# Two transformer blocks on one core: weight chunks issued ahead of the norm vectors' rows, and a later start of the modulation product

## The chip, the cores and the metric

The kernel runs on one core of a Trainium2 chip. The metric is the device time of one execution in microseconds (us); the time before is a median of three runs. An engine is called by its short name: PE is TensorE, DVE is VectorE, ACT is ScalarE, POOL is GpSimd, SP is SyncE, which here issues DMA transfers.

## The reference

Input `x` has 256 rows of 1024 values, fp32. The first block is an RMS norm, one wide product with `w_in` that is cut into ten parts, a recurrent branch and a sparse attention branch, a merge, and a gated FFN. The second block runs two layers with a modulation (`c @ w_mod + b_mod`) of norm outputs, and a second stream of 256 context rows (`ctx`) beside the main rows.

```python
def first_block(x, norm_mix_pre, w_in, ...):
    for l in range(DEPTH):
        h = rms_norm(x, norm_mix_pre[l])
        proj = h @ w_in[l]
        ...
        xr, gr, q, k, v, iq, ik, iw, g_a, g_b = parts
        ...
        iq = partial_rope(iq.reshape(bsz, s, N_IDX_HEADS, IDX_DIM), IDX_ROT_DIM)
        ik = layer_norm(ik, idx_k_ln_g[l], idx_k_ln_b[l])
        ik = partial_rope(ik[:, :, None, :], IDX_ROT_DIM)[:, :, 0, :]
        ...
def second_block(x, c, ctx, c_ctx, w_mod, b_mod, ...):
    for l in range(DEPTH_2):
        mod = (silu_c @ w_mod[l] + b_mod[l])[:, None, :]
        mod_c = (silu_cc @ w_mod[l] + b_mod[l])[None, None, :]
        ...
        h = modulate(x, g_pre_mix[l], sh_m, sc_m)
        hc = modulate(ctx, g_pre_mix[l], csh_m, csc_m)
```

## The kernel before

Every product is fp32 accuracy out of three fp32r matmuls: a weight chunk is loaded raw (`mraw`, up to 128x1024), ACT writes its rounded half `mhi` (L319) and DVE the remainder `mlo` (L320); the activations are split in the same way into `xTh` and `xTl`. `wraw` (L173) issues the load on SP's queue and `wload` (L178) takes a chunk that was loaded ahead, if there is one, and splits it. Three `mraw` buffers and three pairs of halves are in rotation. The instructions of each engine are put in a row by a scheduler that works from the program's order, the dependences and its own estimate of times; engines then run their rows strictly in order.

At the begin SP issues the two tiles of `x` (L92), the constant table `tab` (L94, it holds the identity for transposes, the rope tables and masks) and the rows of seven norm and gate vectors (`columns`, L104 to L118, name `vc`). Each is a DMA of 4 to 16 KB into one 128x128 tile, which PE transposes (L114) and ACT copies (L116). Then come three chunks of `w_in` that are loaded ahead (L613, `ahead`): they are for columns 3584 to 3876, the first half of the index projection `pidx`. DMAs use eight completion semaphores in turn, so each one also waits until the eighth before it has landed. `norm_T` (L614) squares `x` on ACT, takes the power -0.5 on POOL (`rs`, L336), scales on DVE (`xn`, L347), transposes on PE (L354), multiplies with the norm vector on DVE and ACT alternately (`mod`, L369 and L366) and splits into `xTh` and `xTl`. A second set of vector rows, `v2` (L617), holds the condition vector `c`.

The index projection (L683) makes two halves of 292 columns with `prod_x`; ACT evacuates each (L687). Then for both row tiles DVE applies rope to the query part (L509 to L512), and the key part `ik` goes through a layer norm (DVE L696, L699, ACT square, DVE `ms` L334, POOL `rs` L336, DVE L702, L703), rope and a copy (L705); PE transposes both (L711, L716) and multiplies them (L728). The next product is that of k, from column 3072 of `w_in`.

`Side` (L129) hands out steps of a generator: `tick(us)` is called by each product with an estimate of its time, adds it to `due`, and runs a step whenever `due` has reached `every`. The modulation (L519) is such a generator, 49 steps of one 512 KB chunk of `w_mod` (`wraw` tile, L536) and its matmuls (L554) each; it starts at L631 with `every` 4.2 and an extra `tick(8.4)`. During the FFN of the first block the context rows' projection and attention (`ctx_project`, L1238) are the generator, one step per 9.5, started at L1262; `side.finish()` (L1267) runs what is left. In an attention (`attend`), for each pair of heads, stage_a makes scores (L1040) and a softmax on DVE and ACT (`Pm`), and stage_b transposes (L1075), copies (`PTm`) and multiplies with the values (L1088). The boundary (L1275) closes the FFN with a norm and starts the next layer's products. The context's output projection `down_f` (L1291) is 96 matmuls of fhi, flo with cah, cal; the scheduler puts them where it sees room.

```python
    W = T["w_in"][0]
    ahead += [wraw(wview(W, k, min(3, 8 - k), 3584, 292), min(3, 8 - k), 292, "m") for k in (0, 3, 6)]
    xh, xl = norm_T(x, vc[:, O_GM:O_GM + 8], None, "m", "D")
    ...
    side.start(modulation(0, wmx.enter_context(tc.tile_pool(name="wm", bufs=1, side="right")), mods[0]), 4.2)
    side.tick(8.4)
    ...
    side.start(ctx_project(cres), 9.5)
```

Of the kernel before, what the change touches and what calls it, by code (L numbers as in the profile page):

```python
# [59 lines left out]
def tile_two_blocks(ctx: ExitStack, tc: tile.TileContext, T, out, dbg=None):  # L60
    nc = tc.nc
# [16 lines left out]
    def bank(tag, name="pb"):  # L78
        return ps.tile([P, 512], F32, tag=tag, name=name, bufs=NB[tag])
# [21 lines left out]
    mhalf = cst.tile([P, 32], F32, name="mhalf")  # L101
    nc.vector.memset(mhalf, -0.5)

    def columns(name, parts):  # L104
        rows = cst.tile([P, P], F32, tag="rows", name=name + "_r")
        nc.vector.memset(rows, 0.0)
        offs, r = [], 0
        for src in parts:
            n = src.shape[0]
            nc.sync.dma_start(rows[r:r + n, :], src)  # L110
            offs.append(r)
            r += n
        pt = bank("F", name + "_p")
        nc.tensor.transpose(pt[:, :P], rows, ident)  # L114
        cols = cst.tile([P, P], F32, name=name)
        nc.scalar.activation(cols, pt[:, :P], AF.Copy)  # L116
        return cols, offs

    def vrows(a):
        return a.rearrange("(r p) -> r p", p=P)  # L120

    cw = T["conv_w"][0].rearrange("k (r p) -> (k r) p", p=P)
    vc, o1 = columns("vc", [vrows(T["norm_mix_pre"][0]), vrows(T["norm_ffn_pre"][0]), cw,
                            vrows(T["conv_b"][0]), vrows(T["rg_b_a"][0]), vrows(T["rg_b_x"][0]),
                            vrows(T["rg_lambda"][0])])
    O_GM, O_GF, O_CW, O_CB, O_BA, O_BX, O_LAM = o1


    class Side:  # L129

# [25 lines left out]
    side = Side()  # L156
# [16 lines left out]
    def wraw(src, a, b, s):  # L173
        raw = wpool[s].tile([P, CH[s]], F32, tag=s + "raw", name=s + "raw", bufs=RAWB[s])
        nc.sync.dma_start(raw[:, :a * b].rearrange("p (a b) -> p a b", a=a), src)
        return raw
# [17 lines left out]
    def wview(W, k0, kn, c0, n):  # L194
        return W[k0 * P:(k0 + kn) * P, c0:c0 + n].rearrange("(k p) n -> p k n", p=P)
# [143 lines left out]
    def wide(s, name):  # L339
        return (apool[s].tile([P, 8, S], F32R, tag=s + "xTh", name=name + "h"),  # L340
                apool[s].tile([P, 8, S], F32R, tag=s + "xTl", name=name + "l"))
# [34 lines left out]
    def norm_T(src, A, B, s, tag):  # L376
        xh, xl = wide(s, "xT")
        if s == "f":
            t2 = apool[s].tile([P, 2, D], F32, tag="ftmp", name="xn2")
        for i in range(2):  # L380
            t = t2[:, i] if s == "f" else ap_.tile([P, D], F32, tag="mtmp", name="xn", bufs=2)
            norm_tile(src[:, i], i, A, B, s, tag, xh, xl, t)
        return xh, xl
# [36 lines left out]
    def gain_row(src, name, s="m"):  # L420
        g = apool[s].tile([P, D], F32, tag=s + "G", name=name, bufs=1)
        nc.sync.dma_start(g, bc_row(src, D))
        return g
# [90 lines left out]
    def modulation(l, wmp, res, accs=None):  # L514
# [87 lines left out]
        for r_ in range(2):  # L602
            A = cst.tile([P, 2, 8], F32, name=f"A{l}{r_}")
            for f_, og in ((0, O_PM), (1, O_PF)):
# [4 lines left out]
    mods = [[], []]  # L609


    W = T["w_in"][0]
    ahead += [wraw(wview(W, k, min(3, 8 - k), 3584, 292), min(3, 8 - k), 292, "m") for k in (0, 3, 6)]  # L613
    xh, xl = norm_T(x, vc[:, O_GM:O_GM + 8], None, "m", "D")  # L614


    v2, o2 = columns("v2", [T["g_pre_mix_2"].rearrange("l (r p) -> (l r) p", p=P),  # L617
                            T["g_pre_ffn_2"].rearrange("l (r p) -> (l r) p", p=P),
                            vrows(T["we_pool_scale_2"][0]), vrows(T["c_2"][0]), vrows(T["c_ctx_2"])])
    O_PM, O_PF, O_PS, O_C, O_CC = o2  # L620
    assert O_CC == O_C + 8
    sil = cst.tile([P, 16], F32, name="sil")
# [5 lines left out]
                                sil.rearrange("p (r k) -> p r k", r=2), 0.5)  # L628

    wmx = ExitStack()  # L630
    side.start(modulation(0, wmx.enter_context(tc.tile_pool(name="wm", bufs=1, side="right")), mods[0]), 4.2)  # L631
    side.tick(8.4)


    bax = ExitStack()
# [305 lines left out]
    xh, xl, rows = boundary_ffn(dn.y, 0.5, gpost1, vc[:, O_GF:O_GF + 8], None, 2, (lws[:2], lws[2:]))  # L941
# [451 lines left out]
    xh, xl, rows = boundary_ffn(dn.y, 1.0, gain_row(Gm, "gm1"), Af, Bf, 2, (lws[:2], lws[2:]))  # L1393
# [40 lines left out]
```

## Time and profile before

| what | us |
|---|---|
| median of three runs | 1435.92 (1435.72 to 1436.95) |
| the profiled execution | 1434.95 |
| its span in the trace | 1433.2 |
| PE busy | 1377.9 (96%) |
| DVE busy | 1003.7 (70%) |
| ACT busy | 719.7 (50%) |
| POOL busy | 39.1 (3%) |

The span runs from the first to the last instruction of the trace; 1.75 us of the execution lie outside it. The profiled execution was 0.97 us shorter than the median. A line of the timeline gives start, duration, engine, source line, operation, tiles and, in brackets, how long the engine was idle before it and what ended that. Matmul records overlap, since matmuls are pipelined: the distance of two starts is the rate. "SPq" rows are DMA issues on SP. A few matmul records can be missing from a trace.

### The profile page before, as it was taken

To read this page: it belongs to the slowest core of one execution; us is meant where nothing else is said; L and a number is where in the kernel's file an instruction comes from. 1 tells how busy PE (TensorE), PEld (TensorE's weight loads), DVE (VectorE), ACT (ScalarE), POOL (GpSimd) and SP (SyncE) were. 2 spreads that over 40 slices of the span, in tenths; PEclk is the share of its full clock that TensorE was granted. 3 is DMA by queue.
4 is the path that set the end of the run, shared out by engine and by line. 5 is a ranking of instruction groups with operands and counts; after the bars stand their busy time and mean duration, and the time that the engine had idled before them with its cause. 6 is when DMAs were issued, how large, how long until landed. Compare 5 with 4: busy or idle time off the path is not lost.

```text
span 1433.2 us, 25321 instructions
## 1 busy us (share of the span) xinstructions
PE 1377.9 (96%) x9852; PEld 1219.2 (85%) x9852; DVE 1003.7 (70%) x1972; ACT 719.7 (50%) x1330; POOL 39.1 (3%) x58
## 2 busy tenths in 40 slices
PE   6999999999999999989999999999999999999997
PEld 5887888979999987866899999999678866899997
DVE  4877955476666656787778776687888886555555
ACT  4567743445554555667532222322677676444443
POOL 1000000000000000001000000000000000000000
PEclk9999999999999999999999999999999999999999
DMA  7763799957566552631467556666374510256663
GB/s 249 227 178 89 222 280 286 264 176 228 170 179 207 166 157 88 206 111 58 148 201 219 177 178 197 185 204 189 117 233 150 175 45 18 86 177 191 181 187 118
DMA packets 296576, 247.90 MB, mean 173 GB/s; under 512 B 11445, under 2 KB 275257, under 8 KB 296457
## 3 DMA queue, kind: packets, MB, share of 16 engines
q1 hardware_dynamic: 296456, 246.30, 56.5%
q8 instruction: 77, 1.26, 0.4%
q14 instruction: 43, 0.34, 0.1%
HBM read 245.18 MB, written 1.08 MB: 172 GB/s over the span
## 4 chain that ended last, share of the span: by engine, by line
PE 84%; DVE 6%; ACT 4%; DMA 3%; issue 2%; POOL 1%; SPq 0%; POOLq 0%; DVEq 0%; ACTq 0%
PE pb L215 15%; PE pb L220 15%; PE pb L219 15%; PE pb L230 9%; PE pb L234 9%; PE pb L233 9%; PE pb L1088 2%; PE pb L554 2%; PE pb L1040 2%; DMA mraw<-in_w_in_dram 2%; PE pb L1082 1%; DVE mlo L320 1%; PE pb L354 1%; POOL rs L336 1%; ACT mhi L319 1%
## 5 line engine op out<-in xcount | busy, mean ns | idle before, releaser
L320 DVE TENSOR_TENSOR mlo<-mraw,mhi 128x1024 fp32r<-128x1024 f32 (+2 forms) x297 | 360.8, 1218 | 246.4 <-ACT mhi L319 243.1
L319 ACT ACTIVATE mhi<-mraw 128x1024 fp32r<-128x1024 f32 (+2 forms) x297 | 312.1, 1054 | 422.1 <-PE pb L219 199.2
L215 PE MATMUL pb<-xTh,mhi 128*128 128x256 f32 x1616 | 461.2, 285 | 0.0
L220 PE MATMUL pb<-xTh,mlo 128*128 128x256 f32 x1616 | 458.6, 284 | 1.6 <-DVE mlo L320 1.4
L219 PE MATMUL pb<-xTl,mhi 128*128 128x256 f32 x1616 | 458.8, 284 | 0.0
L215 PEld LDWEIGHTS pb<-xTh,mhi 128*128 128x128 f32 x1616 | 309.6, 192 | 12.4 <-issue 7.8
L220 PEld LDWEIGHTS pb<-xTh,mlo 128*128 128x128 f32 x1616 | 309.6, 192 | 3.6 <-DVE mlo L320 2.6
L219 PEld LDWEIGHTS pb<-xTl,mhi 128*128 128x128 f32 x1616 | 309.8, 192 | 2.8 <-DVE xTl L320 0.3
L575 DVE SCALAR_TENSOR_TENSOR acc<-wraw,sst,acc 128x1024 f32<-128x1024 f32 x84 | 104.5, 1280 | 6.2 <-DMA wraw<-in_w_mod_dram 6.0
L230 PE MATMUL pb<-mhi,fh 128*128 128x512 f32 x264 | 104.1, 395 | 0.0
L233 PE MATMUL pb<-mlo,fh 128*128 128x512 f32 x264 | 103.5, 392 | 0.0
L234 PE MATMUL pb<-mhi,fl 128*128 128x512 f32 x264 | 102.9, 390 | 0.0
L230 PE MATMUL pb<-mhi,xTh 128*128 128x256 f32 (+1 forms) x272 | 79.9, 295 | 3.9 <-ACT xTh L319 2.4
L233 PE MATMUL pb<-mlo,xTh 128*128 128x256 f32 (+1 forms) x272 | 80.3, 296 | 1.8 <-DVE mlo L320 1.8
L234 PE MATMUL pb<-mhi,xTl 128*128 128x256 f32 (+1 forms) x272 | 80.8, 297 | 0.0
L320 DVE TENSOR_TENSOR flo<-fraw,fhi 128x512 fp32r<-128x512 f32 x92 | 62.7, 688 | 15.2 <-ACT fhi L319 13.0
L319 ACT ACTIVATE fhi<-fraw 128x512 fp32r<-128x512 f32 x92 | 57.0, 625 | 21.9 <-PE pb L234 11.0
L230 PEld LDWEIGHTS pb<-mhi,xTh 128*128 128x128 f32 x272 | 53.5, 197 | 6.7 <-ACT xTh L319 2.8
L234 PEld LDWEIGHTS pb<-mhi,fl 128*128 128x128 f32 x264 | 49.6, 188 | 11.2 <-DVE fl L320 0.5
L230 PEld LDWEIGHTS pb<-mhi,fh 128*128 128x128 f32 x264 | 49.8, 189 | 10.2 <-ACT fh L319 1.1
L233 PEld LDWEIGHTS pb<-mlo,xTh 128*128 128x128 f32 x272 | 53.5, 197 | 4.5 <-DVE mlo L320 3.0
L233 PEld LDWEIGHTS pb<-mlo,fh 128*128 128x128 f32 x264 | 49.8, 189 | 8.4 <-issue 0.4
(403 smaller groups left out, 2339.9 us busy)
## 6 DMA issues: line engine op xcount, KB each, us to landing
wraw<-in_w_mod_dram SPq DMA_DIRECT2D x96, 512.0 KB
mraw<-in_w_ffn_in_dram SPq DMA_DIRECT2D x84, 512.0 KB
mraw<-in_w_in_dram SPq DMA_DIRECT2D x44, 512.0 KB
mraw<-in_w_ffn_out_dram SPq DMA_DIRECT2D x44, 512.0 KB
mraw<-in_w_ffn_down_dram SPq DMA_DIRECT2D x22, 512.0 KB
fraw<-in_w_ffn_out_dram SPq DMA_DIRECT2D x44, 256.0 KB
mraw<-in_w_ffn_gate_dram SPq DMA_DIRECT2D x20, 512.0 KB
mraw<-in_w_ffn_up_dram SPq DMA_DIRECT2D x20, 512.0 KB
```

The source lines that it names most:

```text
L215: ins = nc.tensor.matmul(dst, wh, xh[:, k], start=(k == 0), stop=False)
L219: nc.tensor.matmul(dst, wh, xl[:, k], start=False, stop=False)
L220: ins = nc.tensor.matmul(dst, wl, xh[:, k], start=False, stop=(k == 7))
L230: ins = nc.tensor.matmul(dst, xh_k, wh, start=first, stop=False)
L233: nc.tensor.matmul(dst, xh_k, wl, start=False, stop=False)
L234: return nc.tensor.matmul(dst, xl_k, wh, start=False, stop=last)
L319: return (nc.scalar.activation(hi, src, AF.Copy), nc.vector.tensor_sub(lo, src, hi.bitcast(F32)))
L320: nc.vector.tensor_sub(lo, src, hi.bitcast(F32)))
L554: ins = nc.tensor.matmul(pb[32 * q:32 * q + 32, h * 256:(h + 1) * 256], lhs, rhs[:, q], start=first, stop=last, tile_position=(0, 32 * q), ...
L575: ins = nc.vector.scalar_tensor_tensor(acc[:, r_], raw, col, acc[:, r_], OP.mult, OP.add)
L1040: nc.tensor.matmul(sb[j][:, n * S:(n + 1) * S], qs[a][hd, i * P:(i + 1) * P], keys[n][b][hd, kv, :], start=(m == 0), stop=(m == 2))
L1088: nc.tensor.matmul(ob[64 * j:64 * j + 64, :S], vals[k // 2](k % 2, kv), pts[j][:, k], start=(k == 0), stop=(k == 2 * nb - 1), skip_group_c ...
```

## The change

It does three things. `columns` takes the queue that issues its rows, and `vc` is given ScalarE's (`nc.scalar`), `v2` keeps SP's. The call for `vc` stands behind the three loads ahead. The modulation starts with `due` at -4.1 and `every` 4.1, in place of an extra tick of 8.4 and `every` 4.2.

```diff
-    def columns(name, parts):
+    def columns(name, parts, queue):
...
-            nc.sync.dma_start(rows[r:r + n, :], src)
+            queue.dma_start(rows[r:r + n, :], src)
...
-    vc, o1 = columns("vc", [vrows(T["norm_mix_pre"][0]), vrows(T["norm_ffn_pre"][0]), cw,
-                            vrows(T["conv_b"][0]), vrows(T["rg_b_a"][0]), vrows(T["rg_b_x"][0]),
-                            vrows(T["rg_lambda"][0])])
-    O_GM, O_GF, O_CW, O_CB, O_BA, O_BX, O_LAM = o1
...
     ahead += [wraw(wview(W, k, min(3, 8 - k), 3584, 292), min(3, 8 - k), 292, "m") for k in (0, 3, 6)]
+    vc, o1 = columns("vc", [vrows(T["norm_mix_pre"][0]), vrows(T["norm_ffn_pre"][0]), cw,
+                            vrows(T["conv_b"][0]), vrows(T["rg_b_a"][0]), vrows(T["rg_b_x"][0]),
+                            vrows(T["rg_lambda"][0])], nc.scalar)
+    O_GM, O_GF, O_CW, O_CB, O_BA, O_BX, O_LAM = o1
...
-                            vrows(T["we_pool_scale_2"][0]), vrows(T["c_2"][0]), vrows(T["c_ctx_2"])])
+                            vrows(T["we_pool_scale_2"][0]), vrows(T["c_2"][0]), vrows(T["c_ctx_2"])], nc.sync)
...
-    side.start(modulation(0, wmx.enter_context(tc.tile_pool(name="wm", bufs=1, side="right")), mods[0]), 4.2)
-    side.tick(8.4)
+    side.start(modulation(0, wmx.enter_context(tc.tile_pool(name="wm", bufs=1, side="right")), mods[0]), 4.1)
+    side.due = -4.1
```

The scheduler answers with new rows on every engine. Lines of the changed kernel are 5 lower up to L608 and 1 lower behind it. Three places matter here.

At the begin, on SP's queue (DMA issues; `mraw` is a chunk of `w_in`, `v_r` holds the rows of `v2`), before:

```order
L110 DMA vc_r<-in_rg_b_x_dram 8x128
L110 DMA vc_r<-in_rg_lambda_dram 8x128
L175 DMA mraw<-in_w_in_dram 128x3x292 x2
L175 DMA mraw<-in_w_in_dram 128x2x292
L110 DMA v_r<-in_g_pre_mix_dram 16x128
L110 DMA v_r<-in_g_pre_ffn_dram 16x128
```

and now, from `tab` on:

```order
L94 DMA tab<-in_c_tab_dram 128x960
L170 DMA mraw<-in_w_in_dram 128x3x292 x2
L170 DMA mraw<-in_w_in_dram 128x2x292
L110 DMA v_r<-in_g_pre_mix_dram 16x128
L110 DMA v_r<-in_g_pre_ffn_dram 16x128
```

The first three chunks of `w_in` stand right behind `tab`. Further on in the same queue (`wraw` is a chunk of `w_mod`, `gp` and `bm` are rows of the modulation), before:

```order
L522 DMA gp<-in_g_post_ffn_dram 2x512 x2
L536 DMA wraw<-in_w_mod_dram 128x4x256 x2
L548 DMA bm<-in_b_mod_dram 2x512 x4
L536 DMA wraw<-in_w_mod_dram 128x4x256
L679 DMA lng<-in_idx_k_ln_g_dram 128x64
L680 DMA lnb<-in_idx_k_ln_b_dram 128x64
L536 DMA wraw<-in_w_mod_dram 128x4x256 x2
L175 DMA mraw<-in_w_in_dram 128x3x292 x2
L175 DMA mraw<-in_w_in_dram 128x2x292
```

and now:

```order
L678 DMA lng<-in_idx_k_ln_g_dram 128x64
L679 DMA lnb<-in_idx_k_ln_b_dram 128x64
L517 DMA gp<-in_g_post_mix_dram 2x512 x2
L517 DMA gp<-in_g_post_ffn_dram 2x512 x2
L531 DMA wraw<-in_w_mod_dram 128x4x256 x2
L170 DMA mraw<-in_w_in_dram 128x3x292 x2
L170 DMA mraw<-in_w_in_dram 128x2x292
L543 DMA bm<-in_b_mod_dram 2x512 x4
```

The second three chunks of `w_in` stand ahead of `bm` and of three of the five `wraw` loads that were ahead of them.

ACT at the begin, before (`sp` is a small table of the recurrent branch):

```order
L327 ACT_TABLE_LOAD
L327 ACTIVATE xn,acc<-x 128x1024 x2
L116 ACTIVATE vc<-vc_p 128x128
L646 ACTIVATE sp_218<-sp_217 128x8
L319 ACTIVATE mhi<-mraw 128x876
L366 ACTIVATE mod<-pb,vc 128x128 x2
L319 ACTIVATE mhi<-mraw 128x876
L319 ACTIVATE mhi<-mraw 128x584
```

and now, from the fifth of the seven vector rows on:

```order
L110 DMA vc_r<-in_rg_b_a_dram 8x128
L110 DMA vc_r<-in_rg_b_x_dram 8x128
L110 DMA vc_r<-in_rg_lambda_dram 8x128
L322 ACT_TABLE_LOAD
L322 ACTIVATE xn,acc<-x 128x1024 x2
L116 ACTIVATE vc<-vc_p 128x128
L314 ACTIVATE mhi<-mraw 128x876
L645 ACTIVATE sp_193<-sp_192 128x8
L314 ACTIVATE mhi<-mraw 128x876
L314 ACTIVATE mhi<-mraw 128x584
L361 ACTIVATE mod<-pb,vc 128x128 x3
```

All seven DMA issues stand ahead of the table load and the two squares of `x`, and all three `mhi` ahead of the multiplication with the norm vector (`mod`).

DVE at the begin, before (`xn` are the two tiles of the scaled `x`):

```order
L334 TENSOR_SCALAR ms<-acc 128x1 x2
L347 TENSOR_SCALAR xn<-x,rs 128x1024 x2
L106 MEMSET v_r 128x128
L644 TENSOR_SCALAR sp_216<-vc 128x8
L661 TENSOR_SCALAR sq_252<-vc 128x8
```

and now:

```order
L644 TENSOR_TENSOR sp_192<-vc,sp_191 128x8
L655 TENSOR_SCALAR sp_191<-sp_191 128x8
L315 TENSOR_TENSOR mlo<-mraw,mhi 128x876
L342 TENSOR_SCALAR xn<-x,rs 128x1024 x2
L646 TENSOR_SCALAR sp_194<-sp_193 128x8
L315 TENSOR_TENSOR mlo<-mraw,mhi 128x876
```

Both `xn` stand behind the small operations on `vc` and behind the first `mlo`, so behind the landing of the vector rows and of the first chunk.

DVE where the index projection ends, before (the `mlo` of 128x1024 is that of the first chunk of columns 3072 and on, `rp` is rope, `pidx` the index projection):

```order
L659 TENSOR_SCALAR sq_250<-sp_216 128x8
L660 TENSOR_SCALAR sq_251<-sp_216 128x8
L320 TENSOR_TENSOR mlo<-mraw,mhi 128x876 x2
L320 TENSOR_TENSOR mlo<-mraw,mhi 128x584
L320 TENSOR_TENSOR mlo<-mraw,mhi 128x1024
L509 TENSOR_TENSOR rp_413<-pidx,tab 128x128
L510 TENSOR_TENSOR rp_414<-pidx,tab 128x8x8
L511 TENSOR_TENSOR rp_414<-pidx,tab 128x8x8
L696 TENSOR_REDUCE lnm<-pidx 128x1
```

and now, at the last part of the `ik` chain, which stood behind that `mlo`:

```order
L505 TENSOR_TENSOR rp_416<-pidx,tab 128x8x8
L704 COPY ik_386<-ik_386 128x64
L506 TENSOR_TENSOR rp_416<-pidx,tab 128x8x8
L702 TENSOR_TENSOR ik_386<-ik_386,lnb 128x64
L507 TENSOR_TENSOR pidx<-rp_415,rp_416 128x8x16
L504 TENSOR_TENSOR rp_434<-ik_386,tab 128x16
L505 TENSOR_TENSOR rp_435<-ik_386,tab 128x8
L506 TENSOR_TENSOR rp_435<-ik_386,tab 128x8
L315 TENSOR_TENSOR mlo<-mraw,mhi 128x1024
L507 TENSOR_TENSOR ik_386<-rp_434,rp_435 128x16
L704 COPY ik_386<-ik_386 128x64
```

The `mlo` of the first 128x1024 chunk is now behind the norm and the rope of both tiles of `ik`. On PE, at the same place, before (L711 transposes `pidx`, the others belong to the k product):

```order
L230 MATMUL pb<-mhi,xTh 128x256 x2
L554 MATMUL pb<-wraw,sst 32x256 x5
L233 MATMUL pb<-mlo,xTh 128x256
L234 MATMUL pb<-mhi,xTl 128x256
L230 MATMUL pb<-mhi,xTh 128x256
L233 MATMUL pb<-mlo,xTh 128x256
L234 MATMUL pb<-mhi,xTl 128x256
L230 MATMUL pb<-mhi,xTh 128x256
L711 MATMUL pb<-tab,pidx 128x128 x2
L233 MATMUL pb<-mlo,xTh 128x256
```

and now (L710 and L715 are the transposes of `pidx` and `ik`):

```order
L229 MATMUL pb<-mhi,xTl 128x292
L710 MATMUL pb<-tab,pidx 128x128 x2
L225 MATMUL pb<-mhi,xTh 128x256 x2
L710 MATMUL pb<-tab,pidx 128x128 x6
L228 MATMUL pb<-mlo,xTh 128x256
L229 MATMUL pb<-mhi,xTl 128x256
L225 MATMUL pb<-mhi,xTh 128x256
L228 MATMUL pb<-mlo,xTh 128x256
L229 MATMUL pb<-mhi,xTl 128x256
L715 MATMUL pb<-tab,ik_386 128x128 x2
```

All eight transposes of `pidx` and the matmuls of L554 that stood in between have moved: the transposes stand ahead of the first matmul with `mlo`, L554 comes later. In between the two halves of the index projection no L554 stands any more (before: 40 matmul records).

PE at the end of the first block's FFN, before (L234 is the last matmul of the FFN's down product, L1075, L1088 and L1040 are steps of the context's attention, L354 transposes of the main rows' norm, fhi and cah belong to the context's output projection):

```order
L234 MATMUL pb<-mhi,fl 128x512
L1075 MATMUL pb<-tab,Pm 128x128 x8
L1088 MATMUL pb<-PTm,kvc 64x256 x4
L1040 MATMUL pb<-kTc_3891,qs 128x256
L1040 MATMUL pb<-kTc_3892,qs 128x256
L1040 MATMUL pb<-kTc_3891,qs 128x256 x2
L1040 MATMUL pb<-kTc_3892,qs 128x256
```

and now (each line one lower; L349 is L354):

```order
L229 MATMUL pb<-mhi,fl 128x512
L1039 MATMUL pb<-kTc_3885,qs 128x256 x2
L1039 MATMUL pb<-kTc_3886,qs 128x256 x2
L1039 MATMUL pb<-kTc_3885,qs 128x256 x3
L1039 MATMUL pb<-kTc_3886,qs 128x256
L1039 MATMUL pb<-kTc_3885,qs 128x256
L349 MATMUL pb<-tab,xn 128x128
L1039 MATMUL pb<-kTc_3885,qs 128x256
L1039 MATMUL pb<-kTc_3886,qs 128x256
L1039 MATMUL pb<-kTc_3885,qs 128x256
L349 MATMUL pb<-tab,xn 128x128 x7
L1074 MATMUL pb<-tab,Pm 128x128 x8
```

The scores of one more head pair (12 matmuls, L1039, that stood inside the FFN) come behind the down product, so two rounds of scores, transposes and values stand there where one and a half stood. Of the 96 matmuls of the context's output projection 48 stood at this boundary and 48 among the next layer's kv and q steps; now 16 stand at the boundary, 40 there and 40 in the attention behind it.

## Rows read from the trace of the kernel before

**Rows 1.** Windows view: length, busy us of PE, PEld, DVE, ACT, POOL, PE clock, DMA

```profile
0.00:50.00 50.00, 37.21 (x252) 31.28 (x253) 28.84 (x109) 23.65 (x47) 5.63 (x12) 1.00 0.81 261
50.00:200.00 150.00, 149.71 (x1151) 124.01 (x1149) 121.54 (x377) 97.27 (x203) 1.51 (x3) 1.00 0.62 181
...
600.00:640.00 40.00, 33.57 (x207) 27.78 (x206) 33.05 (x97) 22.33 (x47) 4.34 (x3) 0.91 0.39 115
```

**Rows 2.** Timeline of SP's queue: start, duration of the issue, what is loaded

```profile
0.74 0.86 SPq L92 DMA_DIRECT2D x<-in_x_dram  x2
...
5.59 0.27 SPq L110 DMA_DIRECT2D vc_r<-in_rg_lambda_dram  x1
6.89 1.47 SPq L175 DMA_DIRECT2D mraw<-in_w_in_dram  x3
...
18.35 4.91 SPq L536 DMA_DIRECT2D wraw<-in_w_mod_dram  x2
```

**Rows 3.** Timeline of ACT at the begin

```profile
0.73 1.28 ACT L327 ACT_TABLE_LOAD   x1 [0.73 <-PEq L1419]
4.35 1.06 ACT L327 ACTIVATE xn<-x 128x1024 f32<-128x1024 f32 x1 [2.33 <-DMA x<-in_x_dram]
...
5.60 1.06 ACT L327 ACTIVATE xn<-x 128x1024 f32<-128x1024 f32 x1
...
10.50 0.93 ACT L319 ACTIVATE mhi<-mraw 128x876 fp32r<-128x876 f32 x1 [0.71 <-DMA mraw<-in_w_in_dram]
```

**Rows 4.** Timeline of DVE: the first `xn`, and parts of the `ik` chain

```profile
6.87 0.75 DVE L347 TENSOR_SCALAR xn<-x,rs 128x1024 f32<-128x1024 f32 x1
...
36.56 1.23 DVE L320 TENSOR_TENSOR mlo<-mraw,mhi 128x1024 fp32r<-128x1024 f32 x1 [3.58 <-ACT mhi L319]
37.70 0.28 DVE L509 TENSOR_TENSOR rp<-pidx,tab 128x128 f32<-128x128 f32 x1
...
40.11 0.22 DVE L699 SCALAR_TENSOR_TENSOR lnc<-lnm,pidx 128x64 f32<-128x64 f32 x1
40.86 0.29 DVE L702 SCALAR_TENSOR_TENSOR ik<-lnc,rs,lng 128x64 f32<-128x64 f32 x1 [0.53 <-POOL rs L336]
...
42.21 0.22 DVE L511 TENSOR_TENSOR rp<-pidx,tab 128x64 f32<-128x64 f32 x1
```

**Rows 5.** Tile view of `rs`, 0 to 60 us: ns min/median/max, first and last start

```profile
L336 POOL TENSOR_TENSOR rs<-ms,mhalf x4: 550/788/1391, 5.8 to 42.6; 128x1 f32<-128x1 f32 x4
```

**Rows 6.** Timeline of PE from its first transposes to those of `pidx`

```profile
8.37 0.45 PE L114 MATMUL vc_p<-tab,vc_r 128*128 128x128 f32 x1 [0.22 <-DMA vc_r<-in_rg_lambda_dram]
...
14.44 0.61 PE L230 MATMUL pb<-mhi,xTh 128*128 128x292 f32 x1 [2.42 <-ACT xTh L319]
...
21.01 0.30 PE L230 MATMUL pb<-mhi,xTh 128*128 128x292 f32 x1
...
21.96 0.30 PE L233 MATMUL pb<-mlo,xTh 128*128 128x292 f32 x1
...
37.99 0.39 PE L233 MATMUL pb<-mlo,xTh 128*128 128x256 f32 x1
...
43.88 0.87 PE L711 MATMUL pb<-tab,pidx 128*128 128x128 f32 x6 [0.38 <-DVE pidx L512]
```

**Rows 7.** Lines view of PE, 20.8 to 38: busy us, mean ns, idle before

```profile
L230 PE MATMUL pb<-mhi,xTh 128*128 128x292 f32 (+1 forms) x26 | 7.6, 304 | 1.4 <-ACT mhi L319 1.4
...
L554 PE MATMUL pb<-wraw,sst 128*32 128x256 f32 x50 | 3.8, 387 | 0.0
```

**Rows 8.** Waits view of PE, 540 to 680 us: us in total, times, longest

```profile
PE pb L1010 <- issue: 3.5, 1, 3.5
PE pb L1010 <- DVE qte L987: 2.5, 1, 2.5
PE pb L1040 <- DVE ms L334: 0.9, 1, 0.9
PE pb L1040 <- ACT Pm L1056: 0.9, 1, 0.9
```

## Prediction, made before the run

> **What bounds the kernel now.** The windows view was read first. PE is busy for 149.71 of the 150 us from 50 to 200 [rows 1], so a change of the begin cannot be hidden by what follows it: each us that the first 50 gain or lose stays, unless it is given back where PE waits again. PE waits in the first 50 us (37.21 busy, so 12.8 idle) and in the next layer's kv and q steps (600 to 640: 33.57 busy, 6.4 idle) [rows 1]. Next come the timelines of the begin. SP issues the last of the seven vector rows at 5.59 and the three `mraw` at 6.89 [rows 2], each behind the landing of an earlier transfer; ACT sits idle for 0.71 us until the first chunk is there at 10.50 [rows 3]; PE starts the first product at 14.44 after 2.42 us without work [rows 6], and at the second half of that product it waits 1.4 us for a chunk [rows 7]. That chunk is late because SP stood from 18.35 to 23.26 at two `wraw` loads, with the `mraw` behind them [rows 2]. These are the waits that the change touches. The last view is that of PE's waits behind the FFN [rows 8].
>
> **The change, part by part.** The sum is made against the profiled execution, 1434.95, which is 0.97 under the median of the runs. A measurement of this kernel can tell some 0.2% from no change, 2.9 us.
>
> *ACT's seven issues.* Before, ACT issues no DMA in any row. Bounds from SP: 0.27 for a vector row and 0.43 for a tile of `x` [rows 2], so 1.9 to 3.0 us for seven; I take the middle, 0.35, since six of the seven wait for nothing. They begin at about 1.0 (an estimate: the table load's 0.73 [rows 3] and the tile's clearing), and the seventh waits for a landing: the row issued at 5.59 released PE at 8.37 [rows 2, 6], 2.8 us, so the first lands at 3.8 and the seventh goes at 4.2. Behind it the table load of 1.28 [rows 3], so the squares of `x` start at 5.5 in place of 4.35 (bounds 4.5 and 6.0).
>
> *The first chunks.* `tab` now waits for the first tile of `x` by its semaphore, as the turn of the semaphores has moved, and is issued at 4.4. That tile took 3.6 us from its issue at 0.74 to 4.35, and the second came 1.25 behind it [rows 2, 3], the rate of 512 KB. So `tab` (480 KB) lands at 8.0 in place of 6.9, and the chunks at 9.1, 10.2 and 10.9; before, the first came at 10.50 [rows 3]. `xn` waits in DVE's row for `mhi` (0.93 [rows 3]) and `mlo` (1.23 for 1024 columns [rows 4], so 1.05 for 876) of the first chunk: 11.05 in place of 6.87 [rows 4]. Before, 7.57 us passed from there to the first product [rows 4, 6]; of these the 0.71 of waiting and the first `mhi` and `mlo` are gone, so 4.9 stay. The first product starts at 15.9, **1.5 later**: the chunks come sooner, but `xn` and `tab` come later.
>
> A rule bears on this. The Trainium skill, DMA: Bandwidth & Descriptors, section "Issuing engines are not separate DMA queues", says that transfers started by different engines run on the same 16 DMA engines and interleave, and that a second issuing engine saves the issuing time alone. By it the gain is at most SP's seven issues, 1.9 to 3.0 us by the bounds above, and only where SP's issuing is what `mraw` waits for; the rows show SP waiting for landings, so the sum by the rule has nothing to gain here either.
>
> *The index projection.* The first 24 matmuls go at a slow pace (14.44 to 21.01, 6.57 us with the first waits), then one per 0.136 (seven from 21.01 to 21.96) [rows 6]; the windows call the clock 1.00 throughout [rows 1]. The two halves have 96: 15.9 + 6.57 + 72 x 0.136 = **32.3**. Nothing stands between them now: the second three chunks are ahead of the `wraw` loads that wait, so the 1.4 us [rows 7] go, and the 50 records of L554 that had run by 38, 3.8 us of PE [rows 7], come later. The pace could rise sooner, as PE no longer stands still for 2.42 us between transposes and product: counted from the first transpose at 11.8, 17 matmuls at 0.11 less each, 1.9 us. Between 0 and 1.9 I take 1.0.
>
> *What is late next.* DVE has the `mlo` of the k product's first chunk behind the norm and ropes of both tiles of `ik`, and PE stands in order behind it. From 32.3: evacuation 0.4; the small operations up to the second centred key, 37.70 to 40.33 less the `mlo` that stood among them, 1.5 [rows 4], so 34.2. Then twice a mean 0.15, POOL's power 0.79 (its median [rows 5]) with 0.2 for the handover, and the product behind it 0.29 [rows 4], in turn, since the second mean stands behind the first product: 2.85, so 37.05. Then ropes and copy up to the query part, 40.86 to 42.43 less that product, and one more of 0.29: 1.55 [rows 4]. Then three of 0.08 and the `mlo`, 1.23: **40.1**. PE has in that time the eight transposes of `pidx` and two matmuls, 1.4 us, so it stands idle for over 6 us, where before it lost 0.38 [rows 6]. Before, it reached the same matmul with `mlo` at 37.99 [rows 6], without the transposes (1.2) and with the 50 of L554. Balance: 40.1 + 3.8 - 37.99 - 1.2 - 0.38 = +4.3, less 1.0 for the pace: **+3.3**. Bounds: power at 0.55 and 1.39 [rows 5] gives -0.5 and +0.6, the pace -0.9 and +1.0, the squares +0.6: +1.9 to +5.5.
>
> *The modulation's steps.* They start later by 12.5 on their own scale and catch up 0.1 in each of 49. Wherever they stand from 50 to 200 they are PE work in a full stretch [rows 1]: 0. The last stands at the same place of PE's row as before.
>
> *The context's steps.* One more round of scores and softmax is left for the end of the FFN. Such a round is exposed there already, and in it PE waits 0.9 for DVE, busy with the main rows' norm, and 0.9 for ACT's exponentials [rows 8]; one more, **+1.8**. 32 of the 96 output matmuls move from there to stretches with waits; PE waits 2.5 for `qte` [rows 8], and two more matmuls than before stand ahead of it: **-0.5**. Bounds for both: -0.5 (main rows' norm hides the round) and +3.5 (twice the round).
>
> Sum: 1434.95 + 3.3 + 1.8 - 0.5 = **1439.5**.
>
> **The rivals.**
> - *No net change.* The begin comes out at +1.9 and the extra round hides behind the main rows' norm: 1434.95 + 1.9 - 0.5 = 1436.4. For it: the pace is a matter of PE's idle time before, and 2.42 us of it go. Against: the `ik` chain runs on DVE, ACT and POOL, which follow PE's pace only once. Chance 0.25.
> - *Faster: the moved output matmuls fill holes.* Place: 600 to 640. Price: the two waits of 3.5 and 2.5 us [rows 8]. With 32 matmuls fewer ahead of the main products, the main rows' DVE work starts sooner by itself, while PE has fills; from the point where it leads by more than the longest of the two waits, 3.5 us, both are gone: 1434.95 + 3.3 - 6.0 = 1432.2, and 1430.9 with the begin at +1.9. Against: the longer one is put down to "issue", no wait that the profile shows. Chance 0.17.
> - *The loads share the engines.* If `tab` and the chunks land together at 10.9, `xn` and all behind it move by 1.8 more: 1441.3. Against: the two tiles of `x`, issued together, landed one after the other [rows 3]. Interleaving, as the same section of the Trainium skill has it, would do this. Chance 0.13.
> - The forecast has 0.45.
>
> **How the numbers follow.** Slower by over 2.9: 0.38 of the forecast's 0.45 (its bounds cross 1438.8) and the third rival's 0.13, 0.51. Within: 0.06 of the forecast, 0.22 of the first rival, 0.02 of the second, 0.30. Faster: 0.01, 0.03 and 0.15, 0.19. The range reaches from within the second rival, leaving out its lower half, to the forecast's upper bounds: 1432.5 to 1443.5.
>
> **What would show it.** In the profile after: squares at 5.5, the first chunk at 9.1, the first product near 15.9, no idle PE between the halves, which end near 32; then 5 to 6 us of idle PE up to 40, with DVE's `pidx` and `mlo` as releasers; and 1 to 3 us more of waits behind the FFN's down product. The prediction is wrong if PE is not idle from 32 to 40, or if 600 to 640 has under 3 us of idle PE.

## The result, and the profile after

The change makes the kernel **slower by 0.74%**: the median of six runs is 1448.90 us (1446.61 to 1450.89), that of the kernel before beside it 1436.94 (six runs, 1435.72 to 1439.80). The ratio on record is 1.0074 [1.0062, 1.0087], 10.6 us of 1436.94; the two medians lie further apart, 12.0 us. The differences below go by such ratios. Forecast were 1439.5 and a range up to 1443.5: the direction is right, the size is not. The profiled execution took 1450.89, so its numbers show a little more than the median.

The page's span and its busy times, kernel after:

```profile
span 1449.1 us, 25324 instructions
...
PE 1382.9 (95%) x9852; PEld 1227.0 (85%) x9852; DVE 1003.1 (69%) x1972; ACT 719.9 (50%) x1330; POOL 37.4 (3%) x58
```

PE does the same 9852 matmuls as before, but takes 1382.9 us for them in place of 1377.9, and it idles 66.2 us in place of 55.3. So two things grew: waits, and the time of matmuls that are the same. The windows view, with the stretches of [rows 1] and two around the end of the first block's FFN (columns as there):

```profile
0.00:50.00 50.00, 32.60 (x208) 28.21 (x209) 31.52 (x122) 25.24 (x50) 4.34 (x12) 0.93 0.68 208
...
545.00:580.00 35.00, 28.87 (x142) 21.65 (x140) 21.71 (x55) 19.27 (x50) 2.22 (x4) 0.81 0.21 61
...
600.00:640.00 40.00, 34.72 (x228) 30.16 (x228) 33.12 (x96) 21.43 (x43) 4.34 (x3) 0.91 0.44 135
```

PE is busy 4.6 us less than before in the first 50, and 50 to 200 is as full as it was (149.75 us busy, [rows 1]), so that loss stays. The granted clock is below 1.00 in both stretches, 0.93 and 0.81. Before, both had 1.00 ([rows 1], and the row below). The 0.93 is partly a matter of the run: e4, an experiment from below with the begin of the kernel before, has 0.93 there too. The row of the kernel before:

```profile
545.00:580.00 35.00, 31.45 (x164) 23.70 (x163) 24.84 (x61) 22.52 (x53) 2.22 (x4) 1.00 0.28 88
```

Where the time went is seen at one landmark in each stage, the start of one of POOL's powers (`rs`, and `hr` at 606), in the profiled executions (POOL's timeline). The last two columns are two experiments from below, each of which keeps one half of the change.

| Stage that ends there | before | after | begin alone (e3) | context alone (e4) |
|---|---|---|---|---|
| first block's mixing | 308.18 | +5.2 | +4.1 | +0.3 |
| its FFN | 555.01 | +2.4 | +3.8 | -2.5 |
| behind the boundary, next kv and q steps | 606.17 | +6.3 | +6.3 | +1.1 |
| the attention after it | 691.11 | +14.0 | +7.8 | +9.1 |
| near the end | 1427.46 | +15.9 | +6.6 | +11 |

Most of the lag comes in two portions, before 308 and between 555 and 691; behind 691 it grows by 1.9. Between 308 and 555 the change and e4 gain 2.7, as a round of scores has left the FFN. (The profiled e3, 1441.56, lies in the upper half of its runs, 1437.80 to 1442.88, and lost 4 us more from 555 to 691 with the boundary's steps where they were before. Its rows show PE at the slow pace there behind the same waits; more on this at the end.)

**The begin.** ACT's timeline, kernel after:

```profile
4.43 0.28 ACTq L110 DMA_DIRECT2D vc_r<-in_rg_lambda_dram  x1
4.74 1.28 ACT L322 ACT_TABLE_LOAD   x1 [4.74 <-DMA vc_r<-in_norm_mix_pre_dram]
6.03 1.06 ACT L322 ACTIVATE xn<-x 128x1024 f32<-128x1024 f32 x1
...
9.84 0.93 ACT L314 ACTIVATE mhi<-mraw 128x876 fp32r<-128x876 f32 x1 [1.33 <-DMA mraw<-in_w_in_dram]
```

The seven issues, the table load and the squares came in the order that the prediction had, the squares at 6.03 (forecast 5.5, bound 6.0), and the first chunk's `mhi` started at 9.84 (forecast 9.1, in place of 10.50 [rows 3]). PE's timeline there, from the first transposes on:

```profile
12.59 3.67 PE L349 MATMUL pb<-tab,xn 128*128 128x128 f32 x16 [4.40 <-DVE xn L342]
...
16.74 0.55 PE L225 MATMUL pb<-mhi,xTh 128*128 128x292 f32 x1 [0.27 <-ACT xTh L314]
...
30.80 0.29 PE L229 MATMUL pb<-mhi,xTl 128*128 128x292 f32 x1
31.73 0.44 PE L710 MATMUL pb<-tab,pidx 128*128 128x128 f32 x2 [0.63 <-DVE pidx L507]
33.71 0.51 PE L225 MATMUL pb<-mhi,xTh 128*128 128x256 f32 x2 [1.54 <-ACT mhi L314]
35.70 1.54 PE L710 MATMUL pb<-tab,pidx 128*128 128x128 f32 x6 [1.48 <-DVE pidx L507]
37.07 0.58 PE L228 MATMUL pb<-mlo,xTh 128*128 128x256 f32 x1
```

The first product starts at 16.74 in place of 14.44 [rows 6]. Its two halves follow each other with one wait, 0.41 us for an `mlo` at 24.68, and the last of their matmuls starts at 30.80. Then come three waits, 3.65 us in all, for DVE's `pidx`, for the k product's first `mhi` and for `pidx` again. None is for the k product's `mlo`: DVE ends it at 37.02 (35.80 and 1.22 us, DVE's timeline), while PE still works on the six transposes in front of the matmul that needs it. These six take 1.54 us, where the same six took 0.87 [rows 6]. The granted clock of 30 to 40 is 0.71 (windows view, below under e5). PE's pace fell behind the waits, and the k product went on at it up to 41.

**The boundary** behind the FFN's down product. PE's waits, 540 to 700 us, kernel after (us in total, times, longest):

```profile
PE pb L1039 <- ACT Pm L1055: 4.8, 3, 2.6
PE pb L1009 <- issue: 3.3, 1, 3.3
PE pb L1009 <- DVE qte L986: 2.0, 1, 2.0
PE pb L1074 <- DVE Pm L1061: 1.6, 2, 1.1
```

In place of the 0.9 for ACT's exponentials and the 0.9 for `ms` [rows 8] PE waits 4.8 for the exponentials (4.0 of it up to 600), and 1.6 for DVE's `Pm` (0.6 before). The two waits at L1009 are somewhat shorter than in [rows 8]. PE's timeline from the last matmul of the down product, kernel after:

```profile
558.82 0.62 PE L1039 MATMUL pb<-kTc,qs 64*128 64x256 f32 x6
562.05 0.62 PE L1039 MATMUL pb<-kTc,qs 64*128 64x256 f32 x3 [2.60 <-ACT Pm L1055]
...
563.58 1.75 PE L349 MATMUL pb<-tab,xn 128*128 128x128 f32 x7
...
566.82 1.54 PE L1074 MATMUL pb<-tab,Pm 128*128 128x128 f32 x6 [1.07 <-DVE Pm L1061]
568.41 2.20 PE L1087 MATMUL pb<-PTm,kvc 128*64 128x256 f32 x8
...
573.61 1.46 PE L1039 MATMUL pb<-kTc,qs 64*128 64x256 f32 x6 [1.45 <-ACT Pm L1055]
575.00 1.97 PE L349 MATMUL pb<-tab,xn 128*128 128x128 f32 x8
...
579.51 2.61 PE L1087 MATMUL pb<-PTm,kvc 128*64 128x256 f32 x8
```

and the same steps in the kernel before (line numbers are one higher there; its L354 is L349 here):

```profile
562.16 0.98 PE L354 MATMUL pb<-tab,xn 128*128 128x128 f32 x7
...
564.28 0.88 PE L1075 MATMUL pb<-tab,Pm 128*128 128x128 f32 x6 [0.60 <-DVE Pm L1062]
565.51 1.56 PE L1088 MATMUL pb<-PTm,kvc 128*64 128x256 f32 x8 [0.36 <-ACT PTm L1077]
573.46 1.09 PE L354 MATMUL pb<-tab,xn 128*128 128x128 f32 x8 [0.49 <-DVE xn L347]
```

Behind the wait of 2.6 us each of these groups takes up to 1.8 times as long: seven transposes 1.75 in place of 0.98, eight 1.97 in place of 1.09, the values 2.20 and 2.61 in place of 1.56. This lasts through both rounds, some 20 us. The granted clock from 574 to 582 is 0.50 in the windows view, the lower of its two levels (1.2 GHz); before the first wait PE had worked nearly without a pause (210.75 us busy of the 211.1 from 346.3 to 557.4, windows view).

```profile
574.00:582.00 8.00, 7.41 (x30) 5.11 (x29) 4.15 (x13) 3.86 (x11) 0.10 (x1) 0.50 0.00 0
```

### The profile page after: what moved, and what is told of

Its sections match the earlier page's. It is cut to its first block, busy times and chain, and to the rows that moved or that the text cites. A ratio compares the mean times of both kernels' runs of the same rounds, so it can differ in the third digit from the quotient of the medians.

```text
span 1449.1 us, 25324 instructions
## 1 busy us (share of the span) xinstructions
PE 1382.9 (95%) x9852; PEld 1227.0 (85%) x9852; DVE 1003.1 (69%) x1972; ACT 719.9 (50%) x1330; POOL 37.4 (3%) x58
## 4 chain that ended last, share of the span: by engine, by line
PE 47%; DVE 5%; ACT 2%; issue 1%; DMA 1%; POOL 1%; DVEq 0%; POOLq 0%; ACTq 0%
PE pb L210 8%; PE pb L214 8%; PE pb L215 8%; PE pb L225 6%; PE pb L228 6%; PE pb L229 6%; PE pb L1087 2%; PE pb L1081 1%; PE pb L1039 1%; PE pb L349 1%; POOL rs L331 1%; DVE mlo L315 1%; ACT PTm L1082 0%; DVE ctxx L388 0%; ACT Pm L1055 0%
```

## The experiments

**Which part costs what: e1 to e4.** The first two split the diff by its lines. e1 is the changed kernel with the modulation started as before, so that the order of the loads and ScalarE's queue alone are left; e2 is the kernel before with the modulation's new start alone.

```diff
-    side.start(modulation(0, wmx.enter_context(tc.tile_pool(name="wm", bufs=1, side="right")), mods[0]), 4.1)
-    side.due = -4.1
+    side.start(modulation(0, wmx.enter_context(tc.tile_pool(name="wm", bufs=1, side="right")), mods[0]), 4.2)
+    side.tick(8.4)
```

> The vector rows are issued by ACT behind the three loads ahead, as in the change; the modulation starts as before (4.2 and the extra tick). Theory A (the later start of the modulation makes nearly all of the loss, through the order that it leads to): PE's row is that of the kernel before but for its first 100 rows, so the first product starts some 2 us later (16.7 in the change, 14.4 before) and part of that is given back by the wait between the halves; 0 to +3 us against before, no idle of 5 us behind the index projection, FFN end as before. Rival B (the vector rows on ACT make the loss): +8 to +12 us.

> The modulation starts later (4.1, due -4.1), the vector rows stay on SP ahead of the chunks. Theory A: PE's row is that of the change, so the extra round at the end of the FFN and the idle behind the index projection are there: +8 to +12 us, at least three quarters of the change's loss. Rival B: 0 to +3 us.

Measured: e1 0.9993 [0.9983, 1.0003], e2 1.0090 [1.0074, 1.0106], 12.9 us, somewhat above its forecast; its interval overlaps that of the change. The new queue and the order of the first loads make no difference that can be told from none, and the later modulation costs all of it. In e1 the first product starts at 16.73, as in the changed kernel, 2.3 later than before, and yet the kernel loses nothing: PE's order from there on is that of the kernel before. The 1.4 us of waiting between the halves [rows 7] is gone, 40 records of the modulation's matmuls (L549) stand there by 30 us, the k product stands ahead of the `ik` chain, and its first matmul with `mlo` starts at 37.89 (37.99 before). From 30 to 50 PE waits 0.8 for `mlo` and 0.4 for `pidx`, in the kernel before 0.6 and 0.4. The rule of the Trainium skill that the prediction cited (DMA: Bandwidth & Descriptors, "Issuing engines are not separate DMA queues") agrees with e1: a second issuing engine gained nothing.

The other two split the loss by its place. The planner that sets the context's steps carries its phase on from the modulation; a shift of its due time by 7.8 at the context's start moves those steps back to where they stood (e3, in the changed kernel), or to where the change puts them (e4, in the kernel before).

```diff
     side.start(ctx_project(cres), 9.5)
+    side.due += 7.8
```

(`-= 7.8` in e4.)

> The change, with 7.8 added to due where the context's steps are started, so that each step of them stands at the FFN chunk where it stood before; the begin is the change's. Theory A1 (begin and context add up): the begin's part alone is left, which the powers of POOL put at +5 at 308 us; +4 to +6 us against before. Rival C (the begin makes it all, the rest is what it pushes along): as slow as the change, +12.

> The kernel before, with 7.8 taken off due where the context's steps are started, so that each step stands one FFN chunk later, as in the change; the begin is that of before. Theory A1: the context's part alone, +6 to +9 us, with PE waits behind the down product and the half clock there. Rival C: 0 to +2 us. The prediction's own size for this part was +1.3.

Measured: e3 1.0023 [1.0013, 1.0034], the begin alone, **+3.3 us**, a little under its forecast; e4 1.0043 [1.0027, 1.0059], the context's steps alone, **+6.2**, as theory A1 had it. (By the medians they are +4.6 and +8.2.) Together 0.66%, and the whole is 0.74 [0.62, 0.87]. The table above shows the same in the profiled executions: e3 loses ahead of 308, e4 behind 555.

**The begin's cause: e5.** If the begin loses because the k product's first `mlo` stands behind the `ik` chain, then putting the k product ahead of it must give the loss back, with the modulation's start as the change has it. e5 is e3 with the k product written ahead of the loop over `ik`; the ropes and means wait for its first `mlo`, the transposes of `pidx` for its matmuls.

```diff
+        pk = prod_x(W, 3072, 256, xh, xl, "m", "D")
...
-            rope_partial(bp, pidx[:, i, 0:512].rearrange("p (h d) -> p h d", d=64), 8, i)
+            rope_partial(bp, pidx[:, i, 0:512].rearrange("p (h d) -> p h d", d=64), 8, i,
+                         los[0])
...
+                    after(ins, mms[i])
...
-        pk = prod_x(W, 3072, 256, xh, xl, "m", "D")
```

> As e3 (the change's begin, the context's steps where they stood before), with the k product put ahead of the norm of ik on DVE and PE: its first mlo stands ahead of the ropes, and the transposes of pidx wait for its matmuls. If the idle behind the index projection is DVE's order, as the prediction has it, the idle of PE between 30 and 40 us falls from 3.6 us to under 1.5 and the time by 2 to 5 us against e3, to 0.997 to 1.000 of the kernel before. If the begin's loss is the later first product alone, it stays at +3 us.

Measured: 1.0004 [0.9991, 1.0017], so 0.19% of the 0.23 are gone (the intervals of e3 and e5 overlap a little). The windows view, 30 to 40 us, first the changed kernel (e3 has 6.24 us of PE and 0.86 there), then e5:

```profile
30.00:40.00 10.00, 6.35 (x33) 5.21 (x31) 6.45 (x32) 5.64 (x12) 1.10 (x2) 0.71 0.36 108
```

```profile
30.00:40.00 10.00, 8.79 (x76) 7.77 (x75) 3.87 (x13) 3.35 (x9) 0.19 (x1) 1.00 0.68 199
```

PE is busy 8.79 us in place of 6.35, and the granted clock stays at 1.00. So the idle time behind the index projection and the pace behind it, and not the late first product (16.70 in e5 too), were the begin's cost. That the `mlo` alone makes this idle time isn't shown, since e5 moved more than it. PE's timeline of e5 (L559 is the modulation's matmuls):

```profile
34.37 1.07 PE L559 MATMUL pb<-wraw,sst 128*32 128x256 f32 x16
37.14 0.39 PE L228 MATMUL pb<-mlo,xTh 128*128 128x256 f32 x1 [0.76 <-DVE mlo L320]
```

The first matmul with `mlo` starts no earlier than in the changed kernel (37.07; e3 38.19). But by then e5 has done 32 records of the modulation, 3.0 us, of which the changed kernel and e3 have none before 47; the transposes of `pidx`, 1.3 us, come later, at full pace, and there is less waiting. Which of these is worth how much isn't separated.

**How much of the context's work to leave for the boundary: e6, e7, e11, e12, e13.** The change leaves two rounds of scores and softmax behind the down product, the kernel before one and a half. The number in `side.start(ctx_project(cres), 9.5)` sets it. e6 is the kernel before with 7.6 (no round left), e7 is e5 with 7.6.

> The kernel before with the context's steps every 7.6 in place of 9.5, so that no round of scores is left for the end of the FFN. If exposed rounds cost waits there and the half clock behind them (e4: one round more, +6), one round less saves waits of PE of 2 to 3 us: 1.000 to 0.997. If the FFN is slowed by denser context steps, slower by 1 to 3 us.

> e5 and e6 in one kernel. If the two parts are independent, the sum of their differences: -2 to -6 us against the kernel before.

Measured: e6 1.0059 [1.0042, 1.0076], e7 1.0057 [1.0040, 1.0074]. Both miss: leaving nothing is no better than leaving two rounds. In e6's profiled execution the end of the FFN comes 7.2 us later (562.17 in place of 555.01), as the round and a half is now PE's work in a stretch without holes, and the stretch from there to the power that stood at 572.06 is only 3.2 us shorter. PE still waits at the boundary: 1.1 us for the main rows' norm and 1.6 for `flo`. e11 leaves one round (9.0), e12 half a round (8.4), both in the kernel before.

> The kernel before with the context's steps every 9.0: one whole round (scores, transposes, values) is left behind the down product; before leaves one and the second half of another, the change two, e6 none. Theory H (the waits for the main rows' norm are there anyway, about one round fits into them for nothing, a second does not, and what is moved into the FFN costs PE its own time): the half round costs its 2 us in the FFN and saves under 1 behind it, 1.000 to 1.002. Theory E (each exposed half round costs waits, so fewer is better, and e6 lost by something else): 0.997 to 0.999.

> The same with 8.4: only the second half of the last round is left. Theory H: between e11 and e6, 1.002 to 1.005. Theory E: 0.995 to 0.998.

Measured: e11 0.9990 [0.9980, 1.0001], e12 1.0022 [1.0010, 1.0034]. e12 is in theory H's range; e11 lies below it, at the top of theory E's. Over the rounds left, 0, half, 1, one and a half, 2, the time goes +0.59, +0.22, -0.10, 0, +0.43%, so with less than a round or a second whole one it is slower. That the norm hides about one round fits these times, but is a reading of them and not shown by itself: the order of the output matmuls changes along with the round. e13 joins the two parts that cost nothing, e1 and 9.0.

> e1 and e11 in one kernel: the vector rows on ACT behind the first chunks, the modulation as before, the context's steps every 9.0. If the two small differences are real and add up (0.9993 and 0.999): 0.9983, below 1 by its interval. If they are noise: 1.000.

Measured: 0.9979 [0.9966, 0.9992], 1435.69 beside 1438.33. This is the only version with its whole interval below the kernel before, by 3 us, at the limit of what a measurement here can tell; its profiled execution was itself its slowest (1438.79), so no row shows where the 3 us would come from.

**Waits, or the pace behind them: e8, e9, e10, e14.** e4 has both. e8 is e4 with 16 transposes of the identity between the two halves of the scores, in the two rounds at the boundary. They write a free bank that nothing reads, and keep PE at work where it would wait; e10 is the same in the changed kernel, e9 is e4 once more, beside them.

```diff
+                if s == "f" and p > 1 and i == 0:
+                    wb = bank("M", "warm")
+                    for r in range(16):
+                        warm = nc.tensor.transpose(wb[:, :P], ident, ident)
+                        if r == 0:
+                            after(warm, ins)
```

> e4 with 16 transposes of the identity into a free PSUM bank put between the two halves of the scores in each of the last two rounds, where PE waited 2.3 and 1.5 us; nothing reads them, the other rows of PE keep their order but for five. Theory P (the waits slow PE's pace for some 20 us behind them, and that is the larger part of the context's loss): the matmuls from 558 to 578 go at the pace that they have in the kernel before, and the time falls by 3 to 6 us against e4, though PE has 32 matmuls more. Theory W (the waits alone and the moved output matmuls make the loss): 0 to +3 us against e4.

> e4 once more, on the chip of e8 for the comparison: 1.003 to 1.006 of the kernel before.

> The change with the same 16 transposes in the last two rounds. Theory P: 3 to 6 us less than the change's 1.0074, so 1.003 to 1.0055. Theory W: 1.0074 or more.

Measured: e8 1.0045 [1.0030, 1.0059], e9 1.0045 [1.0030, 1.0060], e10 1.0066 [1.0054, 1.0078] (the change itself 1.0074). By the times theory P missed: e8 is no faster than e9, and e10 stands between the two theories. The traces say more. PE's timeline of e4:

```profile
556.88 0.62 PE L1040 MATMUL pb<-kTc,qs 64*128 64x256 f32 x3 [2.32 <-ACT Pm L1056]
...
558.27 1.76 PE L354 MATMUL pb<-tab,xn 128*128 128x128 f32 x7
...
563.12 2.35 PE L1088 MATMUL pb<-PTm,kvc 128*64 128x256 f32 x8
...
568.47 1.46 PE L1040 MATMUL pb<-kTc,qs 64*128 64x256 f32 x6 [1.45 <-ACT Pm L1056]
569.86 1.97 PE L354 MATMUL pb<-tab,xn 128*128 128x128 f32 x8
...
574.38 2.61 PE L1088 MATMUL pb<-PTm,kvc 128*64 128x256 f32 x8
```

and of e8 (L1049 are the added transposes):

```profile
553.55 1.96 PE L1049 MATMUL warm<-tab 128*128 128x128 f32 x16
...
556.94 1.09 PE L354 MATMUL pb<-tab,xn 128*128 128x128 f32 x8
...
560.35 0.88 PE L1085 MATMUL pb<-tab,Pm 128*128 128x128 f32 x6 [0.79 <-DVE Pm L1072]
561.58 1.57 PE L1098 MATMUL pb<-PTm,kvc 128*64 128x256 f32 x8 [0.36 <-ACT PTm L1087]
```

In e8 the groups take 1.09, 0.88 and 1.57 us, the kernel before's durations; but the 32 added transposes take 3.9 us themselves. The fill doesn't always keep the pace: in e10's profiled execution the first round falls back to the slow one behind waits of 0.74 and 0.64 us, and only its second is at the full one:

```profile
561.99 1.09 PE L349 MATMUL pb<-tab,xn 128*128 128x128 f32 x8
...
565.39 1.54 PE L1084 MATMUL pb<-tab,Pm 128*128 128x128 f32 x6 [0.64 <-DVE Pm L1071]
566.98 2.61 PE L1097 MATMUL pb<-PTm,kvc 128*64 128x256 f32 x8
```

e14 puts in 8 in place of 16 a round, for half the price.

> e8 with 8 in place of 16 transposes per round, 1 us in place of 2 of each wait filled. Theory P (PE's pace behind the waits is a cost of its own): if 8 are enough to keep the pace, PE saves 2 us of fill against e8 and the time falls below e9's 1.0045 to 1.002 to 1.0035. Theory W (the pace adds nothing to the median): 1.004 to 1.005.

Measured: 1.0021 [1.0009, 1.0032], at the lower end of theory P's forecast and 3.4 us under e9's 1.0045 by the middles; the intervals just touch. The first round is at the slow pace (its wait is still 1.29 us), the second at the full one:

```profile
556.64 0.62 PE L1041 MATMUL pb<-kTc,qs 64*128 64x256 f32 x3 [1.29 <-ACT Pm L1066]
...
558.05 1.76 PE L354 MATMUL pb<-tab,xn 128*128 128x128 f32 x7
...
569.58 1.09 PE L354 MATMUL pb<-tab,xn 128*128 128x128 f32 x8 [0.27 <-DVE xn L347]
```

A sum over the profiled executions holds these together. PE's waits from 540 to 600 are 3.8 us in the kernel before, 5.8 in e4, 4.2 in e8, 4.6 in e14 and 5.6 in e9 (waits view, summed). Slow pace in e4, group by group against the full durations: the transposes of `xn` 0.78 and 0.88, those of `Pm` 0.66 twice, the values 0.78 and 1.04, one group of scores 0.45, the first four output matmuls 0.9 (1.85 in place of 4 x 0.23), 6.1 in all; in e14 the first round's 0.78, 0.66 and 0.78, so 2.2; in e8 none; in e9 the groups of e4 but for the output matmuls, and more of the scores, 6.0 in all.

| | more waits | added transposes | slow pace | sum | lag at 691 |
|---|---|---|---|---|---|
| e4 | 2.0 | 0 | 6.1 | 8.1 | 9.1 |
| e8 | 0.4 | 3.9 | 0 | 4.3 | 4.5 |
| e14 | 0.8 | 2.2 | 2.2 | 5.2 | 5.3 |
| e9 (e4 again) | 1.8 | 0 | 6.0 | 7.8 | 9.7 |

The sums come within 1.0 us of the lags in the first three, and 1.9 short in e9, where the stretch from 606 to 691 is 1.0 longer than in e4. In e4 and e9 the slow pace is the larger part, and PE's busy time on the page says so too: 1384.4 and 1384.8 us for the same 9852 matmuls, 6.5 and 6.9 more than before.

## Why the prediction was wrong in size

**The begin came out as forecast, +3.3 and +3.3 measured (e3), but partly by luck.** The place was right: PE stands idle behind the index projection, and e5, where it doesn't, gives nearly all of the loss back. The terms were less right than their sum. The squares came 0.5 later than forecast and the first product 0.8 (16.74 for 15.9). The pace rose sooner, as was thought possible (from 17.73 on, 0.134 us a matmul), so the halves ended near 31, as forecast with the 1.0 for the pace (31.3). POOL's powers took 0.55 each, the low bound. So PE reached the matmul with `mlo` at 37.07, where the forecast had 39.1 (40.1 less that 1.0), and idled 3.65 us, not over 6. By the prediction's own balance that is 37.07 + 3.8 - 37.99 - 1.2 - 0.38 = +1.3. Two terms that weren't in the sum bring it back. Behind the waits PE's pace fell: a matmul of the k product starts every 0.21 us from 37.4 on, and every 0.12 from 41.3 on, so the clock was still at its lower level when PE had work again (0.50 from 35 to 40, windows view). That is some 1.4 us. And PE waits 0.9 for ACT's `irl` between 45 and 47.3, which it didn't before. The rounds at the boundary add to e3's +3.3 whenever they run at the slow pace, as in its profiled execution, so it isn't the begin's alone.

**The step that failed is "The context's steps", +1.8 and -0.5, so +1.3; measured +6.2 (e4).** By its parts:
- The waits of one more round, +1.8, were about right: 2.0 more in e4's boundary. Their form was not: PE waits 2.3 and 1.45 us at a time. Between the down product and the first of these waits e4 has 6 score matmuls, 0.62 us; before, the last round's transposes and values stood there as well.
- The pace behind those waits was left out, and it is the main part, some 6 us in e4's and e9's profiled executions. The prediction took a changing pace into its sum only as a possible gain at the begin. [Rows 1] gave a hint that it didn't take up: the clock of 0.91 in 600 to 640, the stretch with the waits of 3.5 and 2.5 us [rows 8]. The boundary's own waits before were 0.9 at the longest, and its clock was 1.00.
- The fill, -0.5, did not come. The 32 moved output matmuls left the boundary, 7.4 us at 0.23 each, and came back in full: from the landmark at 606 to that at 691 e4 takes 8.0 us more, and PE's waits in that stretch, 7.8 us before, are 8.0. The bound of +3.5, "twice the round", was drawn from waits alone, and so too low.

How these parts divide the 6.2 over all runs isn't known. The profiled e4 was the slowest of its six runs (1446.0, median 1444.44), but e9's lies in the middle of its six (1444.79, median 1444.43) and has the same slow stretch. Of the twelve runs of the two, four took 1439.9 to 1441.1 us and eight 1443.7 to 1446.0, and both profiled ones are of the longer kind. A pace that falls for a shorter time in the four would explain this, but none of them has a trace, so it isn't shown.

**The rivals.** "No net change" had the extra round hidden by the norm; e4 shows that it isn't (+6.2). "Faster: the moved output matmuls fill holes" fell: both waits at L1010 are still there, 3.2 and 2.0 us in e4. "The loads share the engines" fell as well: the first chunk's `mhi` started at 9.84, not at 10.9. And the late first product, which it would have made later still, costs nothing by itself (e1).

**What would show it**, as listed: no idle PE between the halves (right but for 0.41 us), waits up to 40 with `pidx` and `mlo` as releasers (right for `pidx`; but one of the three is for `mhi` and none for `mlo`, and they make 3.65 us in place of 5 to 6 and end at 35.7), and 1 to 3 us more of waits behind the down product (right: 2.2, as PE's waits from 540 to 600 are 6.0 in place of 3.8). 600 to 640 has 5.3 us of idle PE, over the 3 us set as the mark.

## What to carry to other kernels

A planner's phase is shared state: a start time changed at the begin shifted work 500 us later, and that shift, not the begin, was most of the loss; so hold the later phase fixed when an early step is moved. The amount of side work left for a boundary where the engine waits anyway has a best value, here about one round, with more time on both sides of it: try the neighbouring amounts before judging the move. And don't price a new wait on TensorE by its length alone: compare the durations of the same matmuls behind it with those elsewhere, and in more than one profile, since here they differed between profiles of the same rows.

## What was not expected of the hardware

In the profiled executions of the change, e2, e4 and e9 a wait of 2.3 to 2.6 us was followed by some 20 us at the slow pace, in which PE was again idle for 1.07 and 1.45 us. With 1.09 us of useless transposes in front of the second of these waits the second round ran at the full pace (e14), while the first round, with its wait still at 1.29 us, was slow. But the length of one wait doesn't tell the pace behind it. In the kernel before, waits of 0.94 and 0.92 us left the pace as it was (seven transposes in 0.98 us behind them). In e3, with the same rows of PE and waits of 0.94 and 0.90, the same groups are slow, 2.3 us in three of them; and in e11 a wait of 2.10 us was followed by eight transposes at the full pace. PE's timeline, e3:

```profile
565.73 0.62 PE L1039 MATMUL pb<-kTc,qs 64*128 64x256 f32 x3 [0.90 <-ACT Pm L1055]
566.28 1.75 PE L349 MATMUL pb<-tab,xn 128*128 128x128 f32 x7
```

and e11:

```profile
561.43 1.06 PE L354 MATMUL pb<-tab,xn 128*128 128x128 f32 x8 [2.10 <-DVE xn L347]
```

At the begin the pace is no fixed thing either. The changed kernel and e1 run alike up to the first product (16.74 and 16.73, each behind the same 16 transposes from 12.6 and a wait of 0.27 us), and yet the first reaches the full pace at 17.73 and the second at about 22.3:

```profile
17.73 0.30 PE L225 MATMUL pb<-mhi,xTh 128*128 128x292 f32 x1
```

```profile
17.89 0.44 PE L225 MATMUL pb<-mhi,xTh 128*128 128x292 f32 x1
...
22.32 0.30 PE L225 MATMUL pb<-mhi,xTh 128*128 128x292 f32 x1
```

(the changed kernel, then e1, PE's timeline). What sets the pace in a given run stays open here, and a few us of a single run of this kernel are a matter of that run.

Left open too: which part of the new order makes the idle time at the begin, how the 6.2 us of the context's steps divide over all runs, why e13 is 3 us below the kernel before, and the wait "issue" of 3.3 us at L1009, which no kernel here took away.
